# Where the first norm's feature scale is applied: in the 80 blocks of w_in, or once in x as it is turned

## The chip, the cores and the metric

The kernel runs on one core of one Trainium2 chip. The metric is the device time of one execution in microseconds (us): the median of several executions.

## What is computed

The reference is one inference step of a hybrid decoder layer for 512 prompt rows and 64 sample rows (8 sequences of 8 tokens). Its first step, the only one that the change touches, is a norm and a projection:

```python
def rmsnorm(x, g):
    y = x32 * lax.rsqrt(jnp.mean(x32 * x32, axis=-1, keepdims=True) + EPS)
    return (y * g.astype(jnp.float32)).astype(x.dtype)

proj = rmsnorm(x, lp['g_mix']) @ lp['w_in']
dn_qkv, dn_z, dn_b, dn_a, ssm_u, swa_qkv, lru_x, lru_g = jnp.split(proj, in_split_points(), axis=-1)
...
x = x + concat(A, B, C, D) @ w_out
```

x has 2048 features, w_in has 2048 rows and 5128 columns. The four mixers A (gated DeltaNet), B (an S5 state space model), C (sliding-window attention) and D (RG-LRU) work on slices of proj; x itself, without scale, is added again behind w_out. Two more steps follow in the layer: cross attention and a feed-forward part.

## The kernel before, in words

All 576 rows (512 prompt, 64 sample) are held with the features on the partitions: `xh` and `xl` are 128 partitions x 16 feature groups x 576 columns. A float32 product is made of three products of a reduced type (F32R): `xh` is x rounded to it, `xl` the rest, and each weight block is split into `hi` and `lo` in the same way, so `hi*xh + hi*xl + lo*xh` stands for w*x.

**The start (`first_x`).** Five row tiles `nx` of x are loaded (four of 128 rows, one of 64). TensorE turns each in four groups of 4 x 128 features into a PSUM tile `pm` (L241). ScalarE rounds the PSUM tile into `xh` (L244) and VectorE writes the rest into `xl` (L245): 20 such tiles, 16 of 128x512 and 4 of 128x256. GpSimd squares the first three row tiles (L251, L253) into `nq`, VectorE sums them into `nss` (L254), ScalarE squares the others (L258, `nj`). From the sums come the row factors, spread over the partitions as `rB` (L271, L274). The row factor is applied when a projection is drained; the feature scale `g_mix` (`gmix`, one column for each feature group) cannot be, so it is put into the weights.

**The weight blocks (`block`, `linear`).** w_in is taken in 80 blocks of 4 feature groups x 256 columns: a DMA into `raw` (L119, two buffers), then `hi` and `lo` (two buffers each). With a gain, as for w_in, `hi` and `lo` are made in four pieces of 128x256, each scaled by its own column of `gmix` (L128 on ScalarE, L129 on VectorE); without one, as for w_out and others, in a single 128x1024 instruction each (L123, L124). Each block then has 48 matmuls of 288 columns (L151). The eight small columns of w_in for the DeltaNet gates are a tile of their own, `wb` (L1341 to L1345).

**What sets the order.** Instructions are put in order for each engine ahead of time by a scheduler with priorities (`at(...)`): "first" before "weights" before "drain" before "mix" and "side", and the projection matmuls ("fill") where nothing else is ready. On the chip each engine then takes its own row in that order, and waits for semaphores; SyncE's row (SP) holds all DMAs. While the projections run, the S5 parameters and then the mixers are worked in between.

**x for the residual.** `swa_q` holds, for each of its four column tiles, four calls of `keep_x` (L2031): GpSimd adds `xh` and `xl` into a buffer (L2034) and a DMA writes it to `xd` in DRAM (L2035). `xd` is read when w_out is added (L300).

Of the kernel before, what the change touches and what calls it, by code (L numbers as in the profile page):

```python
# [7 lines left out]
F32 = mybir.dt.float32  # L8
F32R = mybir.dt.float32r
AF = mybir.ActivationFunctionType  # L10
OP = mybir.AluOpType
# [7 lines left out]
class Net:  # L19
# [91 lines left out]
        nc.vector.tensor_tensor(r, r, t, op=OP.mult)  # L111
        return r

    def block(self, w, k0, nk, c0, ncol, gain=None):

        nc = self.nc
        with self.at("weights"):
            raw = self.wp.tile([128, nk, ncol], F32, tag="raw", name="raw", bufs=2)
            nc.sync.dma_start(raw, w[128 * k0:128 * (k0 + nk), c0:c0 + ncol].rearrange("(k p) c -> p k c", p=128))  # L119
            hi = self.wp.tile([128, nk, ncol], F32R, tag="hi", name="hi")  # L120
            lo = self.wp.tile([128, nk, ncol], F32R, tag="lo", name="lo")
            if gain is None:
                nc.scalar.copy(hi, raw)  # L123
                nc.vector.tensor_tensor(lo, raw, hi, op=OP.subtract)  # L124
            else:
                for k in range(nk):
                    g = gain[:, k0 + k:k0 + k + 1]
                    nc.scalar.activation(hi[:, k], raw[:, k], AF.Copy, scale=g)  # L128
                    nc.vector.scalar_tensor_tensor(lo[:, k], raw[:, k], g, hi[:, k], op0=OP.mult, op1=OP.subtract)  # L129
        return hi, lo  # L130

    def linear(self, xh, xl, w, c0, ncol, done, k0=0, nk=None, gain=None):

        nc = self.nc
        nk = nk or xh.shape[1]
        at = (lambda x, k: x[k]) if isinstance(xh, dict) else (lambda x, k: x[:, k])
        step = min(4, nk)
        wide = 1024 // step
        for p in range(0, ncol, wide):
            nm = min(wide, ncol - p) // 128  # L140
            acc = {}
            for kb in range(0, nk, step):
                hi, lo = self.block(w, k0 + kb, step, c0 + p, 128 * nm, gain)
                for m in range(nm):
                    with self.at("fill"):
                        if kb == 0:
                            acc[m] = self.psd.tile([128, 1024], F32, tag="acc", name="acc")
                        for k in range(step):
                            for i, (wt, x) in enumerate(((hi, xh), (hi, xl), (lo, xh))):
                                for j in range(2):  # L150
                                    nc.tensor.matmul(acc[m][:, 224 + 288 * j:512 + 288 * j], wt[:, k, 128 * m:128 * m + 128],  # L151
                                                     at(x, kb + k)[:, 288 * j:288 * j + 288],
                                                     start=(kb + k == 0 and i == 0), stop=(kb + k == nk - 1 and i == 2))
                    if kb + step == nk:
                        with self.at("drain"):
                            done(p // 128 + m, acc[m][:, 224:800])

    def project(self, c0, ncol, done):

        self.linear(self.xh, self.xl, self.a["w_in"][0], c0, ncol, done, gain=self.gmix)  # L160

    def mem_kv(self, mp, ahead):

# [58 lines left out]
    def first_x(self, fp, keep):  # L222

        nc, a = self.nc, self.a
# [10 lines left out]
        for t in range(5):  # L235
            n = 128 if t < 4 else 64
            with self.at("first"):
                for kb in range(0, 16, 4):
                    p = self.pm()
                    for k in range(4):  # L240
                        nc.tensor.transpose(p[:, n * k:n * k + n], xs[t][:, 128 * (kb + k):128 * (kb + k) + 128], self.ident[:n, :n])  # L241
                    p = p[:, :4 * n].rearrange("p (k t) -> p k t", k=4)
                    hi, lo = (z[:, kb:kb + 4, 128 * t:128 * t + n] for z in (self.xh, self.xl))
                    nc.scalar.copy(hi, p)  # L244
                    nc.vector.tensor_tensor(lo, p, hi, op=OP.subtract)  # L245
        for t in range(5):
            n = 128 if t < 4 else 64
            with self.at("mix"):
# [36 lines left out]
class Post(Net):  # L285
# [37 lines left out]
    def row_rstd(self):  # L323
# [6 lines left out]
        for j in range(2):  # L330
# [7 lines left out]
            nc.vector.scalar_tensor_tensor(s[:, c], r[:, c], -0.5, r[:, c], op0=OP.mult, op1=OP.mult)  # L338
            nc.vector.tensor_tensor(s[:, c], s[:, c], v[:, c], op=OP.mult)
            nc.vector.scalar_tensor_tensor(r[:, c], s[:, c], 1.5, r[:, c], op0=OP.add, op1=OP.mult)  # L340

    def halves(self, hi, lo, src):
        self.nc.scalar.copy(hi, src)  # L343
        self.nc.vector.tensor_tensor(lo, src, hi, op=OP.subtract)  # L344

    def cross_open(self, cw):
        nc = self.nc
# [446 lines left out]
class Swa(Post):  # L794
# [41 lines left out]
    def swa_q(self, cv):  # L836
        nc, a = self.nc, self.a

        def done(i, ps):
            for k in range(4):  # L840
                self.keep_x(4 * i + k)
            q = self.nt()
            self.scaled(q, ps, 0.125)
            nc.sync.dma_start(self.qkT[i], q[:, :512])
# [315 lines left out]
class Mix(Swa):  # L1160
# [174 lines left out]
    def delta_ba(self, pool, cv):  # L1335
# [3 lines left out]
        with self.at("weights"):  # L1339
            w = cv.tile([128, 16, 8], F32, name="wb", bufs=1)  # L1340
            nc.sync.dma_start(w, a["w_in"][0][:, 2048:2056].rearrange("(k p) c -> p k c", p=128))  # L1341
            wb = cv.tile([128, 16, 16], F32R, name="wbs", bufs=1)
            nc.vector.tensor_tensor(w, w, self.gmix.unsqueeze(2).to_broadcast([128, 16, 8]), op=OP.mult)
            nc.scalar.copy(wb[:, :, :8], w)
            nc.vector.tensor_tensor(wb[:, :, 8:], w, wb[:, :, :8], op=OP.subtract)  # L1345
        acc = self.psd.tile([128, 1024], F32, tag="acc", name="acc")
# [7 lines left out]
        p = self.pm()  # L1354
# [655 lines left out]
class Full(S5):  # L2010
# [17 lines left out]
        mh, ml = parts or self.w_load(group)  # L2028
        self.linear(mh, ml, a["w_out"][0], 0, 2048, self.add_x(g, first), k0=4 * group, nk=4)

    def keep_x(self, k):  # L2031

        x = self.nt()
        self.nc.gpsimd.tensor_tensor(x, self.xh[:, k], self.xl[:, k], op=OP.add)  # L2034
        self.nc.sync.dma_start(self.xd[k], x)  # L2035

    def sample_step(self, i):

        with self.at("side", (2,)):
# [153 lines left out]
```

## Time and profile before

| what | value |
|---|---|
| time, median of 3 runs | 3059.94 us (3059.22 to 3066.54) |
| profiled execution, its own time | 3060.31 us |
| its span, first to last instruction | 3058.2 us |
| TensorE (PE) busy | 2906.6 us, 95% of the span |
| VectorE (DVE) busy | 2083.6 us, 68% |
| ScalarE (ACT) busy | 1129.0 us, 37% |
| GpSimd (POOL) busy | 1098.4 us, 36% |
| mean granted TensorE clock | 0.985 of full speed |

A busy share is a mean over stages with different limits. TensorE is nearly always busy, so time is won or lost in the stretches in which it waits; each of these is read from the views below. The span lies 2.1 us under the execution's own time.

### The profile page before, as it was taken

How to read it: one execution, taken by the hardware profiler on the slowest of the kernel's cores; microseconds unless marked ns; L12 is line 12 of the kernel's file. 1: busy time of each engine (PE TensorE's matmuls, PEld its weight loads, DVE VectorE, ACT ScalarE, POOL GpSimd, SP SyncE). 2: the span in 40 equal slices, each digit the busy share in tenths (PEclk: the TensorE clock that was granted, in tenths of full speed). 3: DMA queues.
4: the chain of work that ended last, by engine and by line, in shares of the span. 5: the costliest groups of instructions: out<-in, count | busy, mean ns of one | idle time of the engine just before them, and what ended most of it. 6: DMA issues, size and time to landing. Idle time of an engine off the chain costs nothing. (4 is left out here: it accounts for less than half of the span.)

```text
span 3058.2 us, 53977 instructions
## 1 busy us (share of the span) xinstructions
PE 2906.6 (95%) x21347; PEld 2743.7 (90%) x21347; DVE 2083.6 (68%) x3431; ACT 1129.0 (37%) x2013; POOL 1098.4 (36%) x1202
## 2 busy tenths in 40 slices
PE   8988988998999999998899999999999999999998
PEld 8888987887878879987889999999999999999996
DVE  7857756779567575648788888888888853333334
ACT  4433331353423353325344444444444432212214
POOL 4211422313112100102468889888888810000000
PEclk9999999999999999999999999999999999999999
DMA  5465566545576474244323333333333353333322
GB/s 169 133 192 152 163 181 187 166 130 163 166 209 181 136 216 143 68 127 151 118 88 110 107 102 109 107 103 110 106 100 105 113 201 114 101 97 114 107 90 104
DMA packets 370133, 408.41 MB, mean 134 GB/s; under 512 B 37718, under 2 KB 300715, under 8 KB 369176
## 3 DMA queue, kind: packets, MB, share of 16 engines
q1 hardware_dynamic: 369880, 404.96, 43.0%
q8 instruction: 168, 2.75, 0.4%
q14 instruction: 85, 0.70, 0.1%
HBM read 342.85 MB, written 64.69 MB: 133 GB/s over the span
## 5 line engine op out<-in xcount | busy, mean ns | idle before, releaser
L123 ACT CAST hi<-raw 128x1024 fp32r<-128x1024 f32 x158 | 165.6, 1048 | 489.9 <-PE acc L151 425.3
L151 PE MATMUL acc<-xh,hi 128*128 128x288 f32 x1408 | 319.3, 306 | 20.8 <-DVE nt L1192 13.8
L124 DVE TENSOR_TENSOR lo<-raw,hi 128x1024 fp32r<-128x1024 f32 x158 | 195.8, 1240 | 192.0 <-ACT hi L123 186.5
L151 PE MATMUL acc<-xh,lo 128*128 128x288 f32 x1408 | 317.8, 304 | 3.2 <-DVE lo L129 3.1
L151 PE MATMUL acc<-xl,hi 128*128 128x288 f32 x1408 | 317.5, 303 | 2.5 <-DVE xl L245 2.5
L344 DVE TENSOR_TENSOR lo<-S,hi 128x1024 fp32r<-128x1024 f32 x164 | 228.9, 1396 | 89.7 <-ACT hi L343 89.7
L151 PE MATMUL acc<-hh,hi 128*128 128x288 f32 x1280 | 276.1, 297 | 2.8 <-DVE xT L301 2.3
L151 PE MATMUL acc<-hh,lo 128*128 128x288 f32 x1280 | 274.3, 296 | 1.1 <-DVE lo L124 1.1
L151 PE MATMUL acc<-hl,hi 128*128 128x288 f32 x1280 | 275.0, 296 | 0.0
L344 DVE TENSOR_TENSOR al<-raw,ah 128x512 fp32r<-128x512 f32 x328 | 265.1, 844 | 14.2 <-ACT ah L343 14.1
L151 PEld LDWEIGHTS acc<-xh,hi 128*128 128x128 f32 x1408 | 231.8, 192 | 33.9 <-issue 26.6
L343 ACT CAST hi<-S 128x1024 fp32r<-128x1024 f32 x164 | 171.8, 1048 | 211.7 <-POOL S L539 176.9
L151 PEld LDWEIGHTS acc<-xl,hi 128*128 128x128 f32 x1408 | 232.7, 192 | 10.7 <-issue 7.4
L151 PEld LDWEIGHTS acc<-xh,lo 128*128 128x128 f32 x1408 | 231.6, 192 | 10.1 <-issue 4.6
L301 DVE TENSOR_TENSOR xT<-acc,xT 128x576 f32<-128x576 f32 x160 | 120.6, 755 | 168.3 <-PE acc L151 167.0
L536 POOL TENSOR_TENSOR S<-raw 128x256 f32<-128x256 f32 x164 | 168.8, 1029 | 154.5 <-DMA raw<-in_w_up 117.9
L128 ACT ACTIVATE hi<-raw,gmix 128x256 fp32r<-128x256 f32 x320 | 136.5, 498 | 212.8 <-PE acc L151 175.1
L151 PEld LDWEIGHTS acc<-hh,hi 128*128 128x128 f32 x1280 | 206.7, 189 | 3.6 <-ACT hi L123 2.2
L151 PEld LDWEIGHTS acc<-hh,lo 128*128 128x128 f32 x1280 | 207.0, 189 | 1.3 <-DVE lo L124 1.3
L151 PEld LDWEIGHTS acc<-hl,hi 128*128 128x128 f32 x1280 | 207.3, 189 | 0.0
L560 PE MATMUL acc<-Bh,ah 128*128 128x288 f32 x656 | 197.3, 301 | 10.3 <-ACT t L565 10.1
L634 DVE SCALAR_TENSOR_TENSOR y<-ub,vec,y 128x592 f32<-128x592 f32 x176 | 179.9, 1042 | 35.2 <-ACT y L632 34.4
(714 smaller groups left out, 8150.0 us busy)
## 6 DMA issues: line engine op xcount, KB each, us to landing
raw<-in_w_up SPq DMA_DIRECT2D x176, 512.0 KB
raw<-in_w_down SPq DMA_DIRECT2D x88, 512.0 KB
raw<-in_w_in SPq DMA_DIRECT2D x80, 512.0 KB
raw<-in_w_out SPq DMA_DIRECT2D x32, 512.0 KB
hx<-t SPq DMA_DIRECT2D x44, 288.0 KB
ht<-hx SPq DMA_DIRECT2D x44, 288.0 KB
old<-in_cache_win_k SPq DMA_DIRECT2D x48, 256.0 KB
old<-in_cache_win_v SPq DMA_DIRECT2D x48, 256.0 KB
```

Source lines behind the costliest of these rows:

```text
L123: nc.scalar.copy(hi, raw)
L124: nc.vector.tensor_tensor(lo, raw, hi, op=OP.subtract)
L128: nc.scalar.activation(hi[:, k], raw[:, k], AF.Copy, scale=g)
L151: nc.tensor.matmul(acc[m][:, 224 + 288 * j:512 + 288 * j], wt[:, k, 128 * m:128 * m + 128], at(x, kb + k)[:, 288 * j:288 * j + 288], start ...
L301: nc.vector.tensor_tensor(x, ps, old, op=OP.add)
L343: self.nc.scalar.copy(hi, src)
L344: self.nc.vector.tensor_tensor(lo, src, hi, op=OP.subtract)
L536: g(S[:, 0], A(2, 1), A(2, 2), op=OP.add)
L560: nc.tensor.matmul(P[name], wt[:, i, q], xx, start=ch == chs[0] and q == 0 and j == 0, stop=ch == chs[3] and q == 1 and j == 2)
L634: nc.vector.scalar_tensor_tensor(y, u[:, k:k + 592], w(k), y, op0=OP.mult, op1=OP.add)
```

## The change

Four things are done in other places.

1. In `first_x`, VectorE multiplies the PSUM tile by its four columns of `gmix` into a new SBUF tile `xg`, and `xh` and `xl` are made of `xg` by `halves` instead of the PSUM tile. `xg` comes from a pool with one buffer.
2. ScalarE copies each PSUM tile, without scale, into `xr` (four buffers), and a DMA writes it from there to `xd`: 20 DMAs at the start. `keep_x` and its 16 additions and 16 DMAs go.
3. `block` makes every `hi` and `lo` in one instruction of 128x1024.
4. `wb` is no longer multiplied by `gmix` (L1343 goes).

```diff
-    def block(self, w, k0, nk, c0, ncol, gain=None):
+    def halves(self, hi, lo, src):
+        self.nc.scalar.copy(hi, src)
+        self.nc.vector.tensor_tensor(lo, src, hi, op=OP.subtract)
+
+    def block(self, w, k0, nk, c0, ncol):
...
-            if gain is None:
-                nc.scalar.copy(hi, raw)
-                nc.vector.tensor_tensor(lo, raw, hi, op=OP.subtract)
-            else:
-                for k in range(nk):
-                    g = gain[:, k0 + k:k0 + k + 1]
-                    nc.scalar.activation(hi[:, k], raw[:, k], AF.Copy, scale=g)
-                    nc.vector.scalar_tensor_tensor(lo[:, k], raw[:, k], g, hi[:, k], op0=OP.mult, op1=OP.subtract)
+            self.halves(hi, lo, raw)
...
-        self.linear(self.xh, self.xl, self.a["w_in"][0], c0, ncol, done, gain=self.gmix)
+        self.linear(self.xh, self.xl, self.a["w_in"][0], c0, ncol, done)
...
-                    nc.scalar.copy(hi, p)
-                    nc.vector.tensor_tensor(lo, p, hi, op=OP.subtract)
+                    z = fp.tile([128, 512], F32, name="xg")[:, :4 * n].rearrange("p (k t) -> p k t", k=4)
+                    nc.vector.tensor_tensor(z, p, self.gmix[:, kb:kb + 4].unsqueeze(2).to_broadcast([128, 4, n]), op=OP.mult)
+                    self.halves(hi, lo, z)
+
+                    raw = fp.tile([128, 512], F32, name="xr", bufs=4)[:, :4 * n].rearrange("p (k t) -> p k t", k=4)
+                    nc.scalar.copy(raw, p)
+                    with self.at("first"):
+                        nc.sync.dma_start(self.xd[kb:kb + 4, :, 128 * t:128 * t + n].rearrange("k p t -> p k t"), raw)
...
-            for k in range(4):
-                self.keep_x(4 * i + k)
...
-            nc.vector.tensor_tensor(w, w, self.gmix.unsqueeze(2).to_broadcast([128, 16, 8]), op=OP.mult)
...
-    def keep_x(self, k):
-
-        x = self.nt()
-        self.nc.gpsimd.tensor_tensor(x, self.xh[:, k], self.xl[:, k], op=OP.add)
-        self.nc.sync.dma_start(self.xd[k], x)
```

VectorE's row at the start of the program. Before, L245 writes `xl` tile by tile, and the first block's `lo` (L129) comes behind 16 tiles:

```order
L227 MEMSET nss 128x10
L245 TENSOR_TENSOR xl<-pm,xh 128x4x128 x10
L254 TENSOR_REDUCE nss<-nq 128x2
L245 TENSOR_TENSOR xl<-pm,xh 128x4x128 x6
L129 SCALAR_TENSOR_TENSOR lo<-raw,gmix,hi 128x256
L1343 TENSOR_TENSOR wb<-wb,gmix 128x128
L129 SCALAR_TENSOR_TENSOR lo<-raw,gmix,hi 128x256 x3
L245 TENSOR_TENSOR xl<-pm,xh 128x4x64 x2
```

With the change (L242 is the product, L116 the rest, L257 the former L254), from the fourth tile to the seventh:

```order
L242 TENSOR_TENSOR xg<-pm,gmix 128x512
L257 TENSOR_REDUCE nss<-nq 128x2
L116 TENSOR_TENSOR xl<-xg,xh 128x4x128
L242 TENSOR_TENSOR xg<-pm,gmix 128x512
L116 TENSOR_TENSOR xl<-xg,xh 128x4x128
L242 TENSOR_TENSOR xg<-pm,gmix 128x512
L116 TENSOR_TENSOR lo<-raw,hi 128x1024 x2
L116 TENSOR_TENSOR xl<-xg,xh 128x4x128
L242 TENSOR_TENSOR xg<-pm,gmix 128x512
```

Each tile now has two instructions on VectorE with ScalarE's rounding between them, the next product waits for the rest before it (one buffer of `xg`), and the first two blocks' `lo` stand between the sixth tile's product and its rest.

SP's row behind the loads of x. Before, `wb` and the small constants follow the first two blocks, and the S5 parameters (L1684 to L1687) come behind four more blocks:

```order
L119 DMA raw<-in_w_in 128x4x256 x2
L1341 DMA wb<-in_w_in 128x16x8
L1365 DMA dal<-in_dn_a_log 128x4
L1365 DMA dal<-in_dn_dt_bias 128x4
L830 DMA sel<-in_c_sel 128x250
```

With the change:

```order
L123 DMA raw<-in_w_in 128x4x256 x2
L248 DMA xd<-xr 128x4x128 x12
L248 DMA xd<-xr 128x4x64 x4
L1338 DMA wb<-in_w_in 128x16x8
L1680 DMA raw<-in_ssm_a_re 16x128
L1681 DMA raw<-in_ssm_a_im 16x128
L1683 DMA dt<-in_ssm_log_dt 16x2
```

`wb` and the S5 parameters have moved behind the last write of x. TensorE's row at the turning of these parameters, before (L1690) and with the change (L1686):

```order
L151 MATMUL acc<-xh,lo 128x288 x2
L151 MATMUL acc<-xh,hi 128x288
L1690 MATMUL pm<-ident,raw 128x48
L151 MATMUL acc<-xh,hi 128x288
L151 MATMUL acc<-xl,hi 128x288 x2
```

```order
L148 MATMUL acc<-xh,hi 128x288 x2
L148 MATMUL acc<-xl,hi 128x288
L1686 MATMUL pm<-ident,raw 128x48
L148 MATMUL acc<-xl,hi 128x288
L148 MATMUL acc<-xh,lo 128x288 x2
```

Before, 175 projection matmuls stand ahead of it; now 69 do. From the mixers on, TensorE's row is nearly the same in both, and from the feed-forward part on it is the same.

## Rows read from the trace of the kernel before

**Rows 1.** Busy time by stretch: PE, PEld, DVE, ACT, POOL; clock; DMA share; GB/s.
```profile
0.00:25.40 25.40, 14.62 (x88) 11.89 (x88) 15.71 (x25) 17.96 (x39) 15.97 (x13) 0.93 0.76 241
25.40:60.00 34.60, 34.60 (x249) 34.18 (x250) 24.88 (x84) 12.65 (x27) 8.95 (x9) 0.96 0.50 126
60.00:340.00 280.00, 251.47 (x2032) 238.50 (x2031) 212.00 (x511) 106.48 (x221) 61.99 (x64) 0.97 0.49 146
340.00:1130.00 790.00, 736.38 (x5358) 643.39 (x5357) 534.43 (x1008) 282.14 (x613) 178.35 (x172) 0.98 0.60 178
```

**Rows 2.** TensorE in order of time: start, length, [idle before <-releaser].
```profile
25.36 0.61 PE L151 MATMUL acc<-xl,hi 128*128 128x288 f32 x1 [2.47 <-DVE xl L245]
```

**Rows 3.** TensorE's waits in 60 to 1130 us: total us, times, longest.
```profile
PE acc L151 <- DVE nt L1192: 13.8, 5, 6.8
...
PE acc L151 <- DVE lo L129: 3.1, 2, 1.7
...
PE acc L151 <- ACT hi L128: 1.3, 1, 1.3
...
PE pm L1538 <- DVE dw L1560: 0.2, 1, 0.2
```

**Rows 4.** Groups with shapes kept apart, 0 to 1200 us: count, busy us, mean ns.
```profile
L129 DVE SCALAR_TENSOR_TENSOR lo<-raw,gmix,hi 128x256 fp32r<-128x256 f32 x320 | 170.9, 579 | 46.5 <-ACT hi L128 46.1
L128 ACT ACTIVATE hi<-raw,gmix 128x256 fp32r<-128x256 f32 x320 | 136.5, 498 | 212.8 <-PE acc L151 175.1 <-DMA raw<-in_w_in 20.8 <-issue 14.3
...
L124 DVE TENSOR_TENSOR lo<-raw,hi 128x1024 fp32r<-128x1024 f32 x44 | 55.9, 1270 | 15.5 <-ACT hi L123 12.9 <-PE pm L942 1.6
...
L123 ACT CAST hi<-raw 128x1024 fp32r<-128x1024 f32 x44 | 46.0, 1046 | 69.9 <-PE acc L151 49.7 <-DMA raw<-in_w_mem_k 8.1 <-issue 4.1
...
L2034 POOL TENSOR_TENSOR nt<-xh,xl 128x576 f32<-128x576 f32 x16 | 24.1, 1533 | 9.1 <-DVE nt L1389 7.2 <-DVE dco L1194 0.9 <-DMA xd<-nt 0.8
...
L1191 DVE TENSOR_TENSOR nt<-acc,rB 128x512 f32<-128x512 f32 x16 | 10.9, 682 | 0.7 <-PE acc L151 0.7
...
L1059 ACT COPY kt<-pm 128x512 f32<-128x512 f32 x16 | 9.3, 584 | 26.2 <-PE pm L1057 26.2
```

**Rows 5.** The same of VectorE and then of ScalarE, 0 to 60 us.
```profile
L245 DVE TENSOR_TENSOR xl<-pm,xh 128x512 fp32r<-128x512 f32 x16 | 10.2, 685 | 8.9 <-ACT xh L244 8.9
...
L245 DVE TENSOR_TENSOR xl<-pm,xh 128x256 fp32r<-128x256 f32 x4 | 1.5, 405 | 0.0
...
L244 ACT CAST xh<-pm 128x512 fp32r<-128x512 f32 x16 | 8.9, 592 | 5.4 <-PE pm L241 5.4
...
L258 ACT ACTIVATE nj<-nx 128x1024 f32<-128x1024 f32 x2 | 2.1, 1068 | 0.0
L244 ACT CAST xh<-pm 128x256 fp32r<-128x256 f32 x4 | 1.5, 379 | 0.0
```

**Rows 6.** VectorE, then GpSimd, in order of time between 27 and 36 us.
```profile
28.40 3.24 DVE L1345 TENSOR_TENSOR wbs<-wb,wbs 128x128 fp32r<-128x128 f32 x1
...
27.89 3.60 POOL L251 TENSOR_TENSOR nq<-nx 128x2048 f32<-128x2048 f32 x1 [4.26 <-DVE nss L254]
31.57 3.82 POOL L253 TENSOR_TENSOR nq<-nq 128x1024 f32<-128x1024 f32 x2
```

**Rows 7.** VectorE's groups in the feed-forward part, 1500 to 2450 us.
```profile
L344 DVE TENSOR_TENSOR al<-raw,ah 128x512 fp32r<-128x512 f32 x161 | 151.6, 941 | 5.4 <-ACT ah L343 5.2
```

**Rows 8.** SP's queue in order of time, 0 to 60 us.
```profile
5.59 5.64 SPq L1341 DMA_DIRECT2D wb<-in_w_in  x1
...
46.45 0.41 SPq L1687 DMA_DIRECT2D dt<-in_ssm_log_dt  x1
```

**Rows 9.** VectorE's, then TensorE's step on these parameters, in order of time.
```profile
48.08 0.22 DVE L1688 COPY raw<-dt 16x128 f32<-16x128 f32 x1
...
50.85 0.26 PE L1690 MATMUL pm<-ident,raw 48*128 48x48 f32 x1
```

**Rows 10.** Instructions on xd: length ns min/median/max, first and last start us.
```profile
L300 SPq DMA_DIRECT2D nt<-xd x16: 320/338/1477, 860.6 to 944.2; - x16
```

More of the change, by code (lines that the diff above doesn't have):

```diff
@@ L121, in block, with linear @@
             lo = self.wp.tile([128, nk, ncol], F32R, tag="lo", name="lo")
-            if gain is None:
-                nc.scalar.copy(hi, raw)
-                nc.vector.tensor_tensor(lo, raw, hi, op=OP.subtract)
-            else:
-                for k in range(nk):
-                    g = gain[:, k0 + k:k0 + k + 1]
-                    nc.scalar.activation(hi[:, k], raw[:, k], AF.Copy, scale=g)
-                    nc.vector.scalar_tensor_tensor(lo[:, k], raw[:, k], g, hi[:, k], op0=OP.mult, op1=OP.subtract)
+            self.halves(hi, lo, raw)
         return hi, lo
-    def linear(self, xh, xl, w, c0, ncol, done, k0=0, nk=None, gain=None):
+    def linear(self, xh, xl, w, c0, ncol, done, k0=0, nk=None):
         nc = self.nc
@@ L142, in linear @@
             for kb in range(0, nk, step):
-                hi, lo = self.block(w, k0 + kb, step, c0 + p, 128 * nm, gain)
+                hi, lo = self.block(w, k0 + kb, step, c0 + p, 128 * nm)
                 for m in range(nm):
@@ L340, in row_rstd @@
             nc.vector.scalar_tensor_tensor(r[:, c], s[:, c], 1.5, r[:, c], op0=OP.add, op1=OP.mult)
-    def halves(self, hi, lo, src):
-        self.nc.scalar.copy(hi, src)
-        self.nc.vector.tensor_tensor(lo, src, hi, op=OP.subtract)
     def cross_open(self, cw):
```

## The prediction

> **What bounds the kernel now.** I first read the busy time by stretch. TensorE works 34.60 of the 34.60 us from 25.4 to 60, 251.47 of 280 us from 60 to 340 and 736.38 of 790 us from there to 1130, which is the part in which w_in and the mixers run; only the first 25.4 us are different, with 14.62 us of turning and almost no projection in them [rows 1]. So TensorE's matmuls bound the kernel, their number does not change, and only two things can move the time: when their stream begins, and how long TensorE waits after that.
>
> The beginning is read from TensorE in order of time: the stream starts at 25.36 us, released by VectorE's `xl` of the last row tile [rows 2]. From there no wait is seen until after 60 us, so a later start moves all that follows.
>
> The waits come from the list of waits between 60 and 1130 us. VectorE ends 20 groups of them, from 13.8 us down to 0.2 us, 49.6 us in sum; ScalarE ends five with 3.8 us. What names the pieces of w_in itself is small: 3.1 us on `lo` and 1.3 us on `hi` [rows 3]. The rest are drains and mixer steps that wait because VectorE is late. ScalarE's `hi` sits idle 212.8 us, 175.1 of them until TensorE frees a buffer [rows 4]: the blocks are ready ahead of need.
>
> **Lighter blocks.** 320 pieces of `lo` keep VectorE busy 170.9 us and 320 of `hi` keep ScalarE busy 136.5 us. In one instruction a block costs 55.9/44 = 1.27 us and 46.0/44 = 1.05 us by the blocks that have no gain [rows 4]. Times 80 that is 101.6 and 83.6 us, so VectorE is rid of 69 us and ScalarE of 53 us. GpSimd is rid of 24.1 us of additions [rows 4], and L1343 goes. None of this is on the path by itself, since TensorE's work covers it; it pays only through the 53.4 us of waits on the two engines. Between 60 and 1130 us VectorE is busy 212.00 + 534.43 = 746 us [rows 1], and some 62 of the 69 us lie there: 8% of its load. A queue that is two thirds full shortens by more than its load does, so I take a bit over a quarter of the 53.4 us: a gain of 15 us. The lower bound is 8% of the waits, 4 us. The upper is half of them, 27 us, and 8 us of clock: the granted clock in these stretches is 0.97 and 0.98 [rows 1], which is some 24 us lost at the lower level, and waits that vanish may give back a third.
>
> **The chain at the start.** This is the term that speaks against the change. Before, ScalarE rounds one tile while VectorE writes the rest of another. Now each tile is a round trip: VectorE's product into the one `xg`, ScalarE's rounding, VectorE's rest, and only then the next product. The product reads PSUM and SBUF as L1191 does, 0.68 us; the rounding is 0.59 us; the rest 0.69 us by L245 [rows 4, 5]: 1.96 us for a 512-wide tile, 31.4 us for 16. The stream needs the 17th tile too, half as wide: 0.405 + 0.379 + 0.405 = 1.2 us [rows 5]. The first tile can begin at about 7.8 us, since ScalarE's first rounding did. That alone gives 40.4 us.
>
> Into the chain come the other instructions of the two rows. On ScalarE four squares `nj` of about 1.07 us [rows 5], two `hi` of 1.05 us, two `xr` copies that stand ahead of a rounding, 0.58 us each [rows 4], and the table load and root for the row factors; on VectorE two `lo` of 1.27 us, three sums and the small steps of the row factors. That is about 10 and 6 us, of which part lies beside the other engine's half of the trip; I take 8 us, between 4 and 12.
>
> Then GpSimd. The new rest reads two SBUF tiles, where L245 read PSUM and SBUF. The trace has an instruction of that kind in the same stretch: L1345, 128x128, took 3.24 us, from 28.40 to 31.64, while GpSimd's L251 ran from 27.89 to 31.49 [rows 6]. It waited for GpSimd's instruction to end, whereas the 16 L245 took 0.685 us on average beside the same squares [rows 5]. GpSimd's squares are three times 3.60 and about 3.8 us, 22 us in nine instructions. A rest that meets one waits half of it on average, 1.2 us, and some six to nine do, partly in time that the chain loses anyway: 4 us. The other end is the feed-forward part, where the same kind of instruction takes 0.94 us on average [rows 7], 0.25 us more than 0.69: 16 times that is 4 us too if GpSimd were always busy, and nothing if the waits fall beside ScalarE's work. I keep 0 to 8. The Trainium skill (SBUF — State Buffer, section Who interferes with whom) says that a VectorE instruction with two SBUF inputs contends with a GpSimd instruction that reads SBUF, and that the loser waits for the whole instruction. L1345 agrees with it. By that rule at its strictest, with one rest let through between two of GpSimd's nine instructions, the sum would stand at my upper end of 8 us instead of 4.
>
> So the stream begins at 40.4 + 8 + 4 = 52.4 us instead of 25.4: 27 us later, between 44.4 (19 us) and 60.4 (35 us). Nothing else can be run in that time, since all early projection work needs `xh` and `xl`.
>
> **The moved loads.** `wb` and the S5 parameters now stand behind the last of 20 writes of x, so they leave at about 59 to 60 us, when the 20th tile is copied. `wb`'s issue held SP for 5.64 us with the loads of x ahead of it [rows 8]; on a quieter queue I allow 2.4 to 5.64. Three short issues of 0.41 us follow, and before, the step on VectorE came at 48.08, 1.6 us after the issue of `dt` [rows 8, 9]. That puts L1688 at 65 to 69 us. TensorE's turning of these parameters stood at 50.85 and followed at once [rows 9]; now only 69 projection matmuls, some 9 us at the pace of 249 in 34.60 us [rows 1], stand ahead of it, so TensorE reaches it at about 62. What is queued behind it is the whole projection stream. I take a wait of 4 us, between 0 and 7. ScalarE's third `hi` stands behind `wb`'s rounding and would come late at about the same time, so this wait covers it.
>
> **Costed at nothing.** The 20 copies `xr` beyond the two above hide beside VectorE's two instructions of each tile (0.58 against 1.37 us); without that cover they would cost 10 us. The writes of x are first read at 860.6 us [rows 10]. SP's wait for two blocks of `raw` ahead of the fifth write delays no rounding as long as four `xr` buffers last 8 us; if they do not, the chain grows by what is missing.
>
> **The sum.** 27 + 4 - 15 = 16 us more. On the profiled execution's own 3060.3 us (its span and 2.1 us around it, 0.4 us above the median of the runs) that is 3076 us. Its own range is 3069 to 3093. What a measurement of this kernel can tell from no change is about 0.3%, 9 us.
>
> **The rivals.**
> *VectorE's relief outweighs the start (faster).* The drains L1192 and the DeltaNet steps wait behind four pieces of `lo` on VectorE; if shorter blocks free them nearly all, the gain is some 45 us of the 53.4 and 8 us of clock: 3060 + 31 - 53 = 3038. It needs a gain over 40 us to fall below 3051. For it: the largest single group, 13.8 us, is a drain [rows 3]. Against it: the one-piece block holds VectorE 1.27 us at a stretch where a drain could slip in after 0.58 before, and much of the waiting is for chains within a mixer. 17%.
> *The two cancel (within 0.3%).* The chain is at its lower bound (19 us), no wait for the parameters, and a gain of 15 to 20: 3060 to 3064. 20%.
> *The S5 parameter chain becomes the bound.* Its turning has moved 106 matmuls forward in TensorE's row, yet its loads come later; if each later step of it (the products R, the C tiles) is missed as well, TensorE waits another 12 to 15 us around 85 to 130 us: 3090. For it, VectorE is busy 212 of 280 us there [rows 1]; against it, three `lo` where there were twelve pieces in that stretch. 15%.
> The forecast itself, 48%.
>
> Slower by over 0.3%: 48 + 15 = 63%; within: 20%; faster: 17%. The range that leaves out 2 in 10 runs from 3050, just below where the cancelling case ends, to 3095, the upper ends of chain and parameters with little gain (3060.3 + 35 + 7 - 7).
>
> **What would show it.** Right: TensorE's projection stream begins at 48 to 57 us, with product, rounding and rest in turn on two engines; some rests take over 1 us while GpSimd squares; a wait of TensorE at the turning of the S5 parameters; L129's 170.9 us replaced by about 100; fewer waits on VectorE in the mixers. Wrong: a stream that begins before 42 us, or waits on VectorE that fall by more than half.

## The result and the profile after

The changed kernel takes 3084.47 us (median of 4 runs, 3083.42 to 3085.71) where the kernel before took 3059.58 us beside it (4 runs, 3059.01 to 3066.54): a ratio of 1.0073, 95% interval 1.0058 to 1.0088, so it is slower. The forecast was 3076 us with a range of 3050 to 3095 and 63% for slower. The direction held, and so did the mechanism of the loss at the start; the reason given for the gain did not. The time lies 8 us above the forecast. The profiled execution of the changed kernel has a span of 3082.4 us, 24.2 us more than before.

In the changed kernel line numbers are a few lower: the product into `xg` is L242, the rounding L115 and the rest L116 (both in `halves`, which the blocks use too), the copy `xr` L246, the write of `xd` L248, the projection matmul L148.

**The stream begins 34 us later.** TensorE in order of time, to be held against [rows 2]:
```profile
55.55 0.69 PE L238 MATMUL pm<-ident,nx 64*128 64x64 f32 x4 [1.49 <-ACT xr L246]
56.75 0.61 PE L148 MATMUL acc<-xh,hi 128*128 128x288 f32 x1 [0.52 <-ACT xh L115]
...
57.88 1.91 PE L275 MATMUL pm<-diag,one 128*128 128x128 f32 x8
59.44 0.59 PE L148 MATMUL acc<-xl,hi 128*128 128x288 f32 x1
59.82 0.68 PE L148 MATMUL acc<-xh,lo 128*128 128x288 f32 x2
```
The matmul at 59.44 is the one that stood at 25.36 before. That is inside the forecast's bounds for the start (up to 60.4), but outside the 48 to 57 us that it named as a sign of being right. Ahead of it TensorE also has eight small matmuls for the row factors (L275), 1.6 us.

**What fills those 59 us.** VectorE in order of time, two undisturbed tiles first (the columns are start, length, and in brackets the idle time ahead and its releaser), then two beside a square on GpSimd:
```profile
38.60 0.69 DVE L242 TENSOR_TENSOR xg<-pm,gmix 128x512 f32<-128x512 f32 x1
39.98 0.69 DVE L116 TENSOR_TENSOR xl<-xg,xh 128x512 fp32r<-128x512 f32 x1 [0.68 <-ACT xh L115]
40.77 0.69 DVE L242 TENSOR_TENSOR xg<-pm,gmix 128x512 f32<-128x512 f32 x1
...
17.11 4.13 DVE L116 TENSOR_TENSOR xl<-xg,xh 128x512 fp32r<-128x512 f32 x1
...
29.44 4.13 DVE L116 TENSOR_TENSOR xl<-xg,xh 128x512 fp32r<-128x512 f32 x1
```
ScalarE and GpSimd in order of time, at the same places:
```profile
39.33 0.62 ACT L115 CAST xh<-xg 128x512 fp32r<-128x512 f32 x1 [1.07 <-DVE xg L242]
39.85 0.58 ACT L246 COPY xr<-pm 128x512 f32<-128x512 f32 x1
...
17.10 3.60 POOL L254 TENSOR_TENSOR nq<-nx 128x2048 f32<-128x2048 f32 x1 [2.52 <-DVE nss L257]
...
29.43 3.60 POOL L254 TENSOR_TENSOR nq<-nx 128x2048 f32<-128x2048 f32 x1 [4.29 <-DVE nss L257]
```
One round trip goes from 38.60 to 40.77, 2.17 us: product 0.69, rounding 0.62, rest 0.69, and 0.17 us of handing over between them. Each engine waits in turn for the other, as was expected. A rest that begins 0.01 us after a square on GpSimd takes 4.13 us, and ends 0.54 us after the 3.60 us of the square.

**What the blocks cost, and what TensorE waits for.** Groups of instructions, 0 to 1230 us (count, busy us and mean ns, idle time ahead), against [rows 4, 5], and the waits of TensorE in the 1070 us from 94 to 1164 (total us, times, longest), against [rows 3]:
```profile
L116 DVE TENSOR_TENSOR lo<-raw,hi 128x1024 fp32r<-128x1024 f32 x124 | 159.4, 1286 | 65.0 <-ACT hi L115 63.4 <-PE acc L148 0.2
L115 ACT CAST hi<-raw 128x1024 fp32r<-128x1024 f32 x124 | 129.9, 1047 | 284.1 <-PE acc L148 243.5 <-issue 18.4 <-DMA raw<-in_w_mem_v 7.0
...
L116 DVE TENSOR_TENSOR xl<-xg,xh 128x512 fp32r<-128x512 f32 x16 | 20.6, 1286 | 7.7 <-ACT xh L115 7.4
```
```profile
PE pm L1528 <- DVE dw L1547: 8.7, 3, 4.8
PE pm L1458 <- DMA dw<-dn: 8.3, 5, 2.9
PE pm L869 <- DVE nt L881: 7.5, 2, 6.4
PE acc L148 <- DVE lo L116: 7.1, 4, 3.6
PE pm L1880 <- ACT ut L1877: 7.0, 1, 7.0
...
PE acc L148 <- DVE nt L1189: 4.0, 3, 2.5
```
The 124 blocks in one piece stand for the 80 of w_in and the 44 without gain of before, 159.4 us against 170.9 + 55.9, as forecast (about 100 for those of w_in). VectorE's part in the waits is 39.7 us in ten groups (8.7 to 0.3 us) instead of 49.6, ScalarE's 10.5 us instead of 3.8. The largest group of before, the drain (L1192 there, L1189 here), is down from 13.8 to 4.0 us; others have come in its place.

Busy time by stretch, moved by the 34 us against [rows 1] (PE, PEld, DVE, ACT, POOL, clock, DMA share, GB/s):
```profile
0.00:59.40 59.40, 22.30 (x95) 17.24 (x96) 39.74 (x55) 28.37 (x52) 24.92 (x15) 0.63 0.59 192
59.40:94.00 34.60, 33.59 (x237) 32.61 (x237) 25.35 (x120) 9.15 (x16) 9.56 (x28) 0.95 0.56 125
94.00:374.00 280.00, 259.82 (x2095) 246.63 (x2094) 185.64 (x359) 88.57 (x132) 51.45 (x41) 0.97 0.50 150
374.00:1164.00 790.00, 738.70 (x5320) 645.29 (x5319) 493.60 (x877) 256.14 (x483) 167.44 (x159) 0.96 0.57 171
```
In the last two stretches VectorE is rid of 67.2 us (679.2 instead of 746.4), and TensorE is busy 10.7 us more, for only 25 more matmuls. The granted clock is 0.96 in the longest stretch where it was 0.98, which takes part of it. So of the 34 us at the start some 10 come back by the end. Behind the stream's start TensorE is idle 126.7 us instead of 140.8 (span less start and busy time), 14 us less, while its matmuls there take 4 us more. The question for the experiments is which part of the change costs and which gives.

**The moved loads.** SP's, VectorE's and TensorE's rows, against [rows 8, 9]:
```profile
27.85 34.19 SPq L248 DMA_DIRECT2D xd<-xr  x16
63.88 0.37 SPq L1338 DMA_DIRECT2D wb<-in_w_in  x1
...
65.75 0.42 SPq L1683 DMA_DIRECT2D dt<-in_ssm_log_dt  x1
```
```profile
67.70 0.22 DVE L1684 COPY raw<-dt 16x128 f32<-16x128 f32 x1
```
```profile
70.08 0.26 PE L1686 MATMUL pm<-ident,raw 48*128 48x48 f32 x1
```
The parameters come 20 us later than before, at the place that was forecast (65 to 69 us), but TensorE comes to their turning (L1686) only at 70.08 us and does not wait there.

### The profile page after: what moved, and what is told of

Same layout as the page of the kernel before. It is cut to its first block, busy times and chain, and to the rows that moved or that the text cites. A ratio compares the mean times of both kernels' runs of the same rounds, so it can differ in the third digit from the quotient of the medians.

```text
span 3082.4 us, 53568 instructions
## 1 busy us (share of the span) xinstructions
PE 2918.6 (95%) x21347; PEld 2754.0 (89%) x21347; DVE 2031.5 (66%) x3210; ACT 1088.8 (35%) x1793; POOL 1084.6 (35%) x1186
## 5 line engine op out<-in xcount | busy, mean ns | idle before, releaser
L115 ACT CAST hi<-raw 128x1024 fp32r<-128x1024 f32 x238 | 249.4, 1048 | 701.6 <-PE acc L148 614.3
L116 DVE TENSOR_TENSOR lo<-raw,hi 128x1024 fp32r<-128x1024 f32 x238 | 299.4, 1259 | 241.2 <-ACT hi L115 236.7
L148 PE MATMUL acc<-xh,hi 128*128 128x288 f32 x1408 | 323.2, 308 | 5.7 <-DVE nt L1189 4.0
L148 PE MATMUL acc<-xh,lo 128*128 128x288 f32 x1408 | 318.8, 305 | 7.1 <-DVE lo L116 7.1
L148 PE MATMUL acc<-xl,hi 128*128 128x288 f32 x1408 | 317.8, 304 | 0.0
L116 DVE TENSOR_TENSOR lo<-S,hi 128x1024 fp32r<-128x1024 f32 x164 | 224.6, 1369 | 92.6 <-ACT hi L115 92.6
L148 PE MATMUL acc<-hh,hi 128*128 128x288 f32 x1280 | 275.4, 296 | 2.8 <-DVE xT L304 2.2
L148 PE MATMUL acc<-hh,lo 128*128 128x288 f32 x1280 | 273.8, 295 | 1.1 <-DVE lo L116 1.1
L116 DVE TENSOR_TENSOR al<-raw,ah 128x512 fp32r<-128x512 f32 x328 | 265.4, 845 | 13.8 <-ACT ah L115 13.8
L148 PE MATMUL acc<-hl,hi 128*128 128x288 f32 x1280 | 274.3, 295 | 0.0
L148 PEld LDWEIGHTS acc<-xh,hi 128*128 128x128 f32 x1408 | 234.2, 194 | 16.3 <-issue 11.3
L148 PEld LDWEIGHTS acc<-xh,lo 128*128 128x128 f32 x1408 | 233.2, 193 | 16.8 <-DVE lo L116 8.1
L115 ACT CAST hi<-S 128x1024 fp32r<-128x1024 f32 x164 | 171.8, 1047 | 204.6 <-POOL S L538 167.3
L148 PEld LDWEIGHTS acc<-xl,hi 128*128 128x128 f32 x1408 | 233.6, 193 | 8.5 <-issue 7.6
L148 PEld LDWEIGHTS acc<-hh,hi 128*128 128x128 f32 x1280 | 206.2, 188 | 3.6 <-ACT hi L115 2.0
L148 PEld LDWEIGHTS acc<-hh,lo 128*128 128x128 f32 x1280 | 206.4, 188 | 1.3 <-DVE lo L116 1.3
L148 PEld LDWEIGHTS acc<-hl,hi 128*128 128x128 f32 x1280 | 206.6, 188 | 0.0
L559 PE MATMUL pp<-Th,hi 128*128 128x288 f32 x656 | 195.3, 300 | 6.6 <-ACT Th L115 3.6
L559 PE MATMUL acc<-Bl,ah 128*128 128x288 f32 x656 | 195.7, 298 | 5.4 <-DVE Bl L116 5.4
```

The costliest lines, as they stand in the source:

```text
L559: nc.tensor.matmul(P[name], wt[:, i, q], xx, start=ch == chs[0] and q == 0 and j == 0, stop=ch == chs[3] and q == 1 and j == 2)
```

## The experiments

Each kernel ran in four to twelve executions beside the kernel before on the same chip; the intervals are 95%. On the three chips of the experiments the kernel before spread over 3051 to 3073 us, so ratios are compared, and a profile, which is one execution, shows less than they do about the time. "Stream" is the start of the matmul that stood at 25.36 us, from the profile of each.

| kernel | stream, us | ratio to before | interval |
|---|---|---|---|
| changed, in three measurements (5 and 11 are the second and third) | 59.4 | 1.0073, 1.0071, 1.0087 | 1.0049 to 1.0103 |
| 1 two buffers for the product | 49.9 | 1.0037 | 1.0022 to 1.0051 |
| 2 no squares on GpSimd | 55.0 | 1.0062 | 1.0044 to 1.0081 |
| 8 four buffers, no squares on GpSimd | 39.4 | 1.0033 | 1.0017 to 1.0050 |
| 7 store late | 59.0 | 1.0093 | 1.0068 to 1.0117 |
| 4, 12 changed, blocks in four scaled pieces | 60.5 | 1.0102, 1.0111 | 1.0082 to 1.0132 |
| 9 before, with the round trip alone | 60.8 | 1.0097 | 1.0073 to 1.0121 |
| 6 before, with the early store alone | 39.9 | 1.0044 | 1.0029 to 1.0059 |
| 3 before, with lighter blocks alone | 23.4 | 0.9998 | 0.9988 to 1.0008 |
| 10 before, with heavier blocks | 25.6 | 1.0096 | 1.0074 to 1.0117 |

My theory: the round trip at the start sets the loss, and the lighter blocks on VectorE give part of it back. The rivals: the blocks give nothing, and what comes back has another source; or another part (the store, the parameters, GpSimd) carries the loss.

**1. Two buffers for the product.** In the changed kernel:
```diff
-                    z = fp.tile([128, 512], F32, name="xg")[:, :4 * n].rearrange("p (k t) -> p k t", k=4)
+                    z = fp.tile([128, 512], F32, name="xg", bufs=2)[:, :4 * n].rearrange("p (k t) -> p k t", k=4)
...
-                    raw = fp.tile([128, 512], F32, name="xr", bufs=4)[:, :4 * n].rearrange("p (k t) -> p k t", k=4)
+                    raw = fp.tile([128, 512], F32, name="xr", bufs=3)[:, :4 * n].rearrange("p (k t) -> p k t", k=4)
```


> The changed kernel with two buffers of xg (and three of xr instead of four, to make room). Theory, that the chain of product, rounding and rest through the one xg sets the late start: a 512-wide tile goes from 2.17 us to about 1.5 us (VectorE's two instructions of 0.69 us and what it loses to GpSimd), TensorE's stream begins near 47 us instead of 59, and the time falls to about 3073 us. Rival, that the writes of x (ScalarE's copies and the row of DMAs) hold the start: stream and time unchanged, 3084 us.

3074.3 us, 1.0037. VectorE in order of time:
```profile
40.28 0.69 DVE L242 TENSOR_TENSOR xg<-pm,gmix 128x512 f32<-128x512 f32 x1
40.89 0.68 DVE L116 TENSOR_TENSOR xl<-xg,xh 128x512 fp32r<-128x512 f32 x1
41.67 0.69 DVE L242 TENSOR_TENSOR xg<-pm,gmix 128x512 f32<-128x512 f32 x1
```
and the group of the rests, 0 to 60 us:
```profile
L116 DVE TENSOR_TENSOR xl<-xg,xh 128x512 fp32r<-128x512 f32 x16 | 23.2, 1455 | 0.0
```
With the next product ahead of the rest, VectorE no longer waits for ScalarE and a tile takes 1.39 us instead of 2.17. The stream comes 9.5 us earlier, and by the ratios the time falls by at least as much. This is the single buffer's price: 16 x 0.78 us of round trip, less 16 x 0.17 us that the rests now lose more beside GpSimd's squares (1455 ns on average instead of 1286), 9.8 us.

**2. The squares off GpSimd.** In the changed kernel:
```diff
-                if t < 3:
+                if t < 0:
```


> The changed kernel with all five row tiles squared on ScalarE, none on GpSimd. Theory, that about 10 us of the chain are rests that wait for GpSimd's squares: no rest takes over 0.8 us, the stream begins 5 to 9 us earlier in spite of 7.5 us more work on ScalarE, and the time is 3076 to 3080 us. Rival, that ScalarE is the tighter of the two rows: the stream begins later than before this edit and the time is 3088 us or more.

3083.64 us, 1.0062. VectorE's group, 0 to 60 us:
```profile
L116 DVE TENSOR_TENSOR xl<-xg,xh 128x512 fp32r<-128x512 f32 x16 | 11.1, 691 | 13.3 <-ACT xh L115 13.2
```
The rest takes 691 ns on average instead of 1286: without GpSimd's squares the waits are gone, 16 x 0.595 = 9.5 us. The stream comes only 4.5 us earlier, less than the 5 to 9 expected; ScalarE has six more squares of 1.07 us in its row. In the time this is inside the interval; in the profile it is plain.

**3. Lighter blocks alone.** In the kernel before, the scale is left out of the blocks of w_in and of `wb` (it is then nowhere, and the values differ):
```diff
-        self.linear(self.xh, self.xl, self.a["w_in"][0], c0, ncol, done, gain=self.gmix)
+        self.linear(self.xh, self.xl, self.a["w_in"][0], c0, ncol, done)
...
-            nc.vector.tensor_tensor(w, w, self.gmix.unsqueeze(2).to_broadcast([128, 16, 8]), op=OP.mult)
```


> The kernel before, with only the blocks made lighter: the gain is left out of w_in and of wb, and x is not scaled either, so the first norm's feature scale is missing from the result. x goes to DRAM as before. Theory, that the lighter blocks give back some 10 us and the start costs all the rest: 3046 to 3052 us, the stream begins at 25 us as before. Rival, that the lighter blocks give nothing: 3060 us.

3062.46 us, 0.9998 with the narrowest interval of all (12 runs): nothing. My theory falls here. TensorE's waits, 60 to 1130 us:
```profile
PE acc L151 <- DVE nt L1192: 13.8, 5, 7.6
PE pm L1531 <- DVE dw L1550: 11.4, 3, 5.3
...
PE acc L151 <- DVE lo L124: 3.8, 2, 2.0
```
The drain costs 13.8 us as it did before [rows 3], though each block holds VectorE for little more than half the time. VectorE's groups add up to 56.7 us of waits, more than the 49.6. How that can come about is read at the longest of these drains, the only one looked into. VectorE in order of time in the kernel before, where TensorE waits 6.8 us:
```profile
234.57 1.64 DVE L1932 TENSOR_TENSOR H<-rt,rt 128x512 f32<-128x512 f32 x1
...
236.36 4.46 DVE L129 SCALAR_TENSOR_TENSOR lo<-raw,gmix,hi 128x256 fp32r<-128x256 f32 x4
240.74 0.68 DVE L1191 TENSOR_TENSOR nt<-acc,rB 128x512 f32<-128x512 f32 x1
...
241.47 2.32 DVE L1925 TENSOR_TENSOR_SCAN G<-M,G 128x512 f32<-128x512 f32 x2
```
and at the same place with lighter blocks, where it waits 7.6 us:
```profile
230.52 1.53 DVE L1931 TENSOR_TENSOR H<-rt,rt 128x512 f32<-128x512 f32 x1
231.97 2.28 DVE L124 TENSOR_TENSOR lo<-raw,hi 128x1024 fp32r<-128x1024 f32 x1
234.17 2.28 DVE L1924 TENSOR_TENSOR_SCAN G<-M,G 128x512 f32<-128x512 f32 x1
236.37 0.66 DVE L1191 TENSOR_TENSOR nt<-acc,rB 128x512 f32<-128x512 f32 x1
```
The block's part is down from 4.46 to 2.28 us, and a scan of the S5 mixer of 2.28 us stands ahead of the drain, where scans came behind it before. The instructions are in another order, and VectorE is busy throughout in both.

The time hides two parts. TensorE's line on the page of the kernel before, and of this one (spans 3058.2 and 3060.2 us):
```profile
PE 2906.6 (95%) x21347; PEld 2743.7 (90%) x21347; DVE 2083.6 (68%) x3431; ACT 1129.0 (37%) x2013; POOL 1098.4 (36%) x1202
...
PE 2914.3 (95%) x21347; PEld 2752.4 (90%) x21347; DVE 2025.8 (66%) x3190; ACT 1076.4 (35%) x1773; POOL 1114.3 (36%) x1202
```
TensorE is idle 145.9 us instead of 151.6, but the same 21347 matmuls take 7.7 us more, beside a mean granted clock of 0.981 instead of 0.985. These are single profiles.

**4 and 12. The changed kernel with the blocks in four scaled pieces again** (the scale is in twice, and the values differ); number 11 is the changed kernel beside it on one chip:
```diff
...
+                for k in range(nk):
+                    g = gain[:, k0 + k:k0 + k + 1]
+                    nc.scalar.activation(hi[:, k], raw[:, k], AF.Copy, scale=g)
+                    nc.vector.scalar_tensor_tensor(lo[:, k], raw[:, k], g, hi[:, k], op0=OP.mult, op1=OP.subtract)
...
```


> The changed kernel with the blocks of w_in made in four scaled pieces as before (the scale is then applied twice). Theory, that the start costs 34 us and the lighter blocks give back 10: stream begins at 57 to 62 us, time 3090 to 3096 us. Rival, that the moved order of the S5 stage gave the 10 us back, not the lighter blocks: 3084 us.

> The changed kernel once more, beside the three below on one chip, so that they can be held against it. Theory: 1.006 to 1.008 of the kernel before. Against the variant with four-piece blocks (1.0102 in the first batch) it tells whether the lighter blocks give anything when they stand behind the later start: if they do, it stays near 1.007; if they give nothing, as the run with lighter blocks alone said, it can come out at 1.009 to 1.010 as well.

> The changed kernel again, on one chip with the next one, which differs from it in the blocks alone. By the first two batches 1.0065 to 1.008 of the kernel before.

> The changed kernel with the blocks of w_in in four scaled pieces again (the scale is in twice and the outputs differ; all else is as in the changed kernel). Theory: behind the later start the lighter blocks give some 5 to 10 us, since heavier blocks cost 29 us where lighter ones gave nothing, so the load is felt on this side: 1.009 to 1.011, 0.2 to 0.3% above the run beside it. Rival: lighter blocks give nothing here either, as in the kernel before, and the difference between 1.0102 and 1.0073 was that of two chips: then both runs of this batch lie within 0.1% of each other.

Number 4 gave 3096.01 us, 1.0102, the changed kernel in the next batch 3082.29 us, 1.0071, then 3088.26 us (1.0087) and number 12 beside it 3093.46 us (1.0111). The difference is 5.2 us on one chip, and 9 to 10 us between the ratios of the other runs; each pair's intervals overlap. Behind the later start lighter blocks may give some 5 us; it is not clear of the noise.

**6. The early store alone.** In the kernel before, with `keep_x` and its additions gone:
```diff
                     nc.vector.tensor_tensor(lo, p, hi, op=OP.subtract)
+                    raw = fp.tile([128, 512], F32, name="xr", bufs=4)[:, :4 * n].rearrange("p (k t) -> p k t", k=4)
+                    nc.scalar.copy(raw, p)
+                    with self.at("first"):
+                        nc.sync.dma_start(self.xd[kb:kb + 4, :, 128 * t:128 * t + n].rearrange("k p t -> p k t"), raw)
...
-            for k in range(4):
-                self.keep_x(4 * i + k)
...
```


> The kernel before with one part of the change alone: x is copied from PSUM and written at the start, and the 16 additions on GpSimd and their writes are gone. Blocks, parameters' scale and the two halves of x stay as before, so there is no product and no round trip. Theory: the copy shares ScalarE with the rounding, 0.59 + 0.58 us for each 512-wide tile against VectorE's 0.69, so the start is bound by ScalarE: 17 tiles by 1.17 us are 20 us, plus 7.8 us for the first and some 6 us of other work: the stream begins near 33 us, 8 us later, and the time is some 6 to 9 us more, 1.002 to 1.003. Rival: the early order of the writes and the additions that are gone give the 10 us back that the changed kernel got back, and the time is 3 to 8 us less than before.

3072.73 us, 1.0044, above both numbers. The store alone makes the start 14.5 us later, not 8, and hardly anything comes back. TensorE, then ScalarE, in order of time:
```profile
22.80 3.68 PE L241 MATMUL pm<-ident,nx 128*128 128x128 f32 x16 [9.54 <-ACT xr L248]
...
31.80 3.80 PE L241 MATMUL pm<-ident,nx 128*128 128x128 f32 x16 [4.84 <-ACT xr L248]
```
```profile
31.16 0.58 ACT L248 COPY xr<-pm 128x512 f32<-128x512 f32 x1 [4.91 <-DMA xd<-xr]
```
The two waits add up to 14.4 us, about the 14.5. The copy keeps the PSUM tile from being reused until ScalarE comes to it. In ScalarE's row four of the copies stand behind squares and two blocks (from 14.23 to 22.18 us), so TensorE's turning waits 9.5 us; later a copy waits 4.9 us for an `xr` buffer: the write that frees it was issued at 25.88 us, behind two loads of w_in in SP's queue.

**7. The store late.** In the changed kernel the copies and the 20 writes go and `keep_x` is back in the first projection (it writes x with the scale in it, so the values differ):
```diff
...
-                    nc.scalar.copy(raw, p)
...
+            for k in range(4):
+                self.keep_x(4 * i + k)
...
```


> The changed kernel with the store put back where it was: no copies from PSUM and no writes at the start, GpSimd adds the two halves in the first projection and writes them (what it writes is x with the scale in it, so the outputs differ from the reference; the work is the same). Theory: the 20 copies and 20 issues stand beside the round trip and cost 2 to 4 us at the start (the two copies ahead of a rounding, and the loads of the S5 parameters), so the stream begins near 56 us instead of 59.4 and the time is 2 to 4 us less than the changed kernel's. Rival one: the copies hide wholly, and the time is the same. Rival two: what the changed kernel got back, some 10 us, came from the additions and writes that were gone from the first projection; then this kernel is 5 to 10 us slower than the changed one.

3090.13 us, 1.0093; the stream begins at 59.0 us instead of 59.4. At the start the store is hidden behind the round trip, as rival one had it. Rival two stays open: on this chip the median lies 7.8 us above the changed kernel's (3082.29), as it forecast, but the intervals of the ratios overlap. Against it stands number 6, in which the additions are gone as well and 13 to 14 of the 14.5 us arrive at the end.

**8. The start mended.** In the changed kernel, `bufs=4` for the product and the edit of number 2:

> The changed kernel with four buffers for the product instead of one, and with the squares of all five row tiles on ScalarE, which frees VectorE's rest of GpSimd. Theory: the two mendings of the first batch gave some 10 and 4.5 us at the stream's start; if they add, the stream begins near 45 us instead of 59.4, 20 us later than before, and the time is 1.001 to 1.003 of the kernel before. Rival: with the squares there too ScalarE has 20 x (0.59 + 0.58) us and ten squares of 1.07 us, 34 us in all, and is the new bound: then the start does not move past that of the two-buffer variant, 49.9 us, and the time is 1.003 to 1.005.

3068.66 us, 1.0033. The stream begins at 39.4 us, earlier than expected, 20 us ahead of the changed kernel, and by the ratios 12 us of that arrive at the end. It is where the store alone begins (39.9): once the round trip is short, ScalarE's roundings, copies and squares set the start. ScalarE is busy 31.31 of the 32.30 us from 7.6 to 39.9:
```profile
7.60:39.90 32.30, 17.66 (x85) 14.37 (x84) 25.86 (x49) 31.31 (x64) 0.00 (x0) 0.65 0.94 292
```

**9. The round trip alone.** In the kernel before (the scale is in twice, and the values differ):
```diff
-                    nc.scalar.copy(hi, p)
-                    nc.vector.tensor_tensor(lo, p, hi, op=OP.subtract)
+                    z = fp.tile([128, 512], F32, name="xg")[:, :4 * n].rearrange("p (k t) -> p k t", k=4)
+                    nc.vector.tensor_tensor(z, p, self.gmix[:, kb:kb + 4].unsqueeze(2).to_broadcast([128, 4, n]), op=OP.mult)
+                    self.halves(hi, lo, z)
```


> The kernel before with one part of the change alone: the turned tile goes through the product into the one buffer, the rounding and the rest. The blocks stay in four scaled pieces (so the scale is in twice and the outputs differ; the work is that of the parts named), the parameters stay early, the store stays in the first projection. Theory: the round trip alone sets the later start, since the variant without the early store began at 59.0 us; the stream begins at 57 to 60 us here. For the end there are two cases. If the 10 us that every late kernel got back by the end came from lighter blocks or from the absent additions, nothing is given back here, and the time is 3091 to 3095 (1.011). If a later start itself gives them back, because what runs beside the stream (loads, early mixer work) is then further along when the stream needs it, the time is 3080 to 3085 (1.007).

3091.5 us, 1.0097: the round trip alone gives the whole later start (60.8 us) and some 30 us of time, by the intervals no less than the whole change. The ratio lies between the two cases of its expectation; with 35 us at the start and 30 at the end, some 5 us come back by themselves, which is within the noise.

**10. Heavier blocks.** In the kernel before two of the four rests of each block are computed twice:
```diff
                     nc.vector.scalar_tensor_tensor(lo[:, k], raw[:, k], g, hi[:, k], op0=OP.mult, op1=OP.subtract)
+                    if k < 2:
+                        nc.vector.scalar_tensor_tensor(lo[:, k], raw[:, k], g, hi[:, k], op0=OP.mult, op1=OP.subtract)
```


> The kernel before with two of the four rests of each block of w_in computed twice: 160 more instructions of 0.53 us on VectorE, 85 us, about as much more as the change took away (the outputs stay the same). Nothing at the start changes but two of VectorE's rows. Theory that the load of the blocks on VectorE lies off the path (as the run with lighter blocks alone says): the time is within 0.3% of before, 3055 to 3067. Rival, that the waits grow with the load as my prediction had it (8% less load, a quarter of the waits): 11% more load gives at least a third more of the waits on VectorE, 17 us and more: 3075 or above, 1.005.

3088.14 us, 1.0096: the rival's number, not the theory's. The added group on VectorE, and TensorE's waits, 60 to 1130 us:
```profile
L131 DVE SCALAR_TENSOR_TENSOR lo<-raw,gmix,hi 128x256 fp32r<-128x256 f32 x160 | 84.7, 537 | 0.0
```
```profile
PE acc L153 <- DVE nt L1194: 17.8, 6, 8.2
PE acc L153 <- DVE lo L131: 12.2, 8, 4.9
PE pm L1886 <- ACT ut L1883: 9.0, 1, 9.0
```
The 84.7 us are felt: `lo` itself now makes TensorE wait 12.2 us where it was 3.1, the drain 17.8 where it was 13.8. But waits are only half of the cost. TensorE's line on the page:
```profile
PE 2917.2 (95%) x21347; PEld 2756.1 (89%) x21347; DVE 2144.0 (70%) x3591; ACT 1128.2 (37%) x2013; POOL 1100.8 (36%) x1202
```
Of the 23 us by which the profiled span is longer, 12.4 are idle time of TensorE (164.0 us instead of 151.6), and 10.6 are the same 21347 matmuls taking longer, beside a lower granted clock: 0.975 to 0.978 in all six executions, 0.980 to 0.987 in those of the kernel before. So in this kernel lighter blocks gave nothing and heavier ones cost 28 us.

## Why the prediction was right, and where its terms were off

**The stream's start, forecast 27 us (19 to 35), measured 34.1.** The mechanism is shown: the round trip alone makes it (number 9), and a second buffer takes 10 us of it away (number 1). Its parts, from the changed kernel's rows:
- The first product starts at 7.76 us, as forecast (7.8).
- A tile takes 2.17 us, not 1.96: the forecast added three durations and left out the 0.17 us of handing over and 0.03 us of the rounding. For 16 tiles that is 3.3 us.
- GpSimd: 16 rests take 1286 ns on average instead of 691 (number 2), 9.5 us, where I took 4 and a bound of 8. The estimate let a rest that meets a square wait half of it. But the squares of the second and third row tile begin right behind VectorE's sum L257 (2.52 and 4.29 us idle until it), and VectorE's next instruction is a rest: both start together, and the rest waits for the whole 3.60 us. The Trainium skill (SBUF — State Buffer, section Who interferes with whom), by which the loser waits for the whole instruction, agrees: 4.13 us at 17.11 and 29.44.
- The other instructions in the two rows: the products stand at 7.76 for the first tile and 55.84 for the 17th, 48.1 us apart. Less 16 x 2.17 and 9.5 that leaves 3.9 us, where I took 8: 1.8 at the two `lo`, 2.0 at the steps of the row factors.
- Not in the sum: three projection matmuls and the eight matmuls L275 that stand ahead of the stream in TensorE's row, with which 2.3 us pass between the end of the 17th tile's rest (57.15) and the stream.

From 7.8 these make 7.8 + 34.7 + 9.5 + 3.9 + 1.3 (the 17th tile) + 2.3 = 59.5 us. In the forecast the two errors of the chain's terms, the round trip and GpSimd too small and the other work too large, partly cancelled.

**The wait for the S5 parameters, forecast 4 us, measured none.** The step on VectorE came when forecast, at 67.70 us, and that is luck: `wb`'s issue began at 63.88 us, 4 us later than I had it, and took 0.37 us, not 2.4 to 5.64. What failed is the other side: I had TensorE at the turning at 62 us, by 9 us of matmuls behind a start at 52.4. The stream began 7 us later, and its matmuls up to the turning took 10.6 us, so TensorE came there at 70.08 us and the data were there first.

**The lighter blocks, forecast a gain of 15 us.** By the profile TensorE is idle 14 us less behind the start, close to the 15, and 4 us of that go to longer matmuls, so 10 us come back. But the reason given is not borne out. Alone, lighter blocks give nothing (number 3, 0.9998). Behind the later start they may give some 5 us (numbers 11 and 12); the additions and writes that left the first projection may give as much (number 7); and number 9, which has neither, gets some 5 us back. None of the three is clear of the noise, so where the 10 us come from stays open, and that the size of the term came near is no proof of its reason. The step that failed is "a queue that is two thirds full shortens by more than its load does": number 3 took the same load away and VectorE's waits did not shrink. VectorE's row is a fixed order, not a queue in which any shorter item brings all others forward; at the longest drain, the one that was read, the block's 2.2 us less were taken by a scan that the new order put there.

With these the sum is 34 + 0 - 10 = 24 us, which is what the spans say; the forecast's 27 + 4 - 15 was 16. The start was 7 us too short and the gain 5 us too large; the wait that did not come took 4 us of these errors back.

**Costed at nothing.** The 20 copies hide behind the round trip, as forecast: without them the start is 0.4 us earlier (number 7). I priced the loss of this cover at 10 us; it is 14.5 (number 6): a copy also holds its PSUM tile (9.5 us), and waits for a buffer behind loads in SP's queue (4.9 us).

**The rivals.** VectorE's relief outweighing the start needed a gain over 40 us: the whole change gave back 10, and number 3 nothing. The two cancelling needed a start of 19 us; it was 34. The S5 chain as the bound did not show: from 85 to 164 us TensorE is idle 1.5 us, not 12 to 15. A cheaper start is what numbers 1 and 8 approach, and they stay above the kernel before. What would beat it was not found: by number 3 even a start without cost would end about level, though no run had the old start, the lighter blocks and no additions together. What stays open is whether a lighter VectorE gives a little behind the late start, and why, if it gives nothing with the early one; the orders of VectorE's row differ in all of these kernels, and no run changed the load under one order.

## What to carry to other kernels

Before work is moved from a covered place to a start that nothing covers, write out the round trip for one tile with its buffers: one buffer between two engines turned 1.39 us of work for a tile into 2.17, and that 10 us reached the end in full. Test each part of a change alone in both directions: here the load that was to be saved was worth nothing when it was taken away, and 85 us more of it cost 28 us, so the busy share of an engine gave neither number. An instruction added to an engine that looks idle can still hold back what another engine needs: TensorE waited 9.5 us for PSUM tiles that were held for a copy. And a longer time need not be waiting alone: of the heavier blocks' 23 us in the profile, 10.6 were the same matmuls taking longer.

## What was not expected of the hardware

A rest of VectorE with both inputs in SBUF that starts together with a square on GpSimd takes 4.13 us instead of 0.69, and in the changed kernel the program's own dependence lets the two start together, at 17.10 and 29.43 us. Two buffers make this worse, not better: the same 16 rests took 1455 ns on average instead of 1286 while the whole start became shorter. The granted clock has a mean of 0.63 up to 59.4 us, while TensorE turns a tile and waits for the next. The stream's first matmuls then run at the lower of the two levels (1.2 GHz; granted clock 0.50 from 59.5 to 62.8 us), two in 0.68 us, and from about 63 us at the upper one (1.00), two in 0.42. The kernel before did the same, from 25.4 to 28.6 us, so this was next to no cost of the change. Less expected is the clock in number 10: only VectorE got more work, and all six executions had a lower mean clock than any of the kernel before.
